# Eight more buffers for modulation weights, a later zero fill, an earlier query projection, and expert lists made beside expert blocks

## The chip, the cores and the metric

The kernel runs on one core of a Trainium2 chip. A core has a matrix engine (TensorE, here PE), a vector engine (DVE), a scalar engine (ACT), a general engine (GpSimd, here POOL) and an engine that mostly issues transfers (SyncE, here SP); sixteen DMA engines move data for all of them. Each engine works through its own list of instructions in order and waits where an operand, a buffer or a transfer is not ready. The metric is device time in microseconds of one execution, lower is better. The kernel before takes 1429.2 us, the median of three runs (1427.99 to 1431.35).

## The reference

One block of a diffusion model with a context prefix: 512 latent and 256 context tokens of width 1024, all in fp32. A conditioning vector gives scales and shifts for each token stream:

```
m = silu(cvec) @ w[:, : n * D_MODEL] + b[: n * D_MODEL]
```

The normalised and modulated tokens are projected by one wide matrix to keys, values, queries, gates and decays. Two mixers run on them, both in both directions of the sequence, and each starts from the state that the context leaves: a retention with a fixed decay per head, and a gated DeltaNet in chunks of 128, which passes the projections through a convolution of three taps and solves a unit lower triangular system in every chunk:

```
a = jnp.einsum('bhnid,bhnjd->bhnij', kc, kc) * bc * jnp.where(strict, jnp.exp(jnp.where(strict, rel, 0.0)), 0.0)
rhs = jnp.concatenate([bc * vc, bc * jnp.exp(g)[..., None] * kc], axis=-1)
sol = lax.linalg.triangular_solve(a + jnp.eye(CHUNK, dtype=a.dtype), rhs,
                                  left_side=True, lower=True, unit_diagonal=True)
```

The merged result goes through an output projection. Then a second normalisation, a router that picks 8 of 64 experts for each token (from 4 of 8 groups), the experts (gate, up and down matrices of width 256), and a shared expert whose output is added.

## The kernel before

Every fp32 product is made of three matmuls, from a high and a low part of each operand (mm3, lines 110 to 113: L111 high by high, L112 and L113 with the low parts). A weight that comes from memory is cast to its high part (hi_of: L100 on ACT, L102 on POOL) and subtracted for its low part (lo_of, L107 on DVE or POOL). Five parts follow one another in the program: the modulation and norms (phase0), the projections and the DeltaNet (phaseG), the retention and the merge (phaseR), the output projection and the router (phaseO), and the experts (phaseM).

The program text is not the order on the engines: a scheduler takes the instructions, puts each on its engine as early as it thinks its operands and buffers are there, and inserts the waits. A buffer is freed by its last reader; a transfer also waits for an earlier one that uses the same completion counter. The counters serve the transfers of SP and ACT in turn.

phase0 loads sixteen pieces of the modulation matrix, wm, 512 KB each (L300, SP), into five buffers. phaseG then casts the projection weights (raw to wu), projects the retention's keys and values from the context (hTc; results rcA and rcB), the gates (gT, L434) and the DeltaNet's keys (kx, kc), which go through conv. The solution of the triangular systems is built by prep, chunk by chunk (CT, M), then by a long chain of small DVE steps for all chunks at once (L569 to L577), written to memory (zd) with zeros where its blocks do not reach, and read back as Z (L582, used at L586). zd is filled with zeros by one transfer (L382) from a small tile.

phaseM holds the experts. Each expert's block on PE is 48 matmuls for gate and up, transposes of the gathered tokens for later experts, and 8 down matmuls (L1258). Weights come three experts ahead. Each expert takes up to 64 tokens in its own slot list; the tokens above 64 go to further lists. Ranks (posm, over, ext) say which tokens those are, and extra makes the first of these lists from them by one-hot matmuls (L1370) with the columns colx. Both are made ahead of the loop over experts.

Of the kernel before, what the change touches and what calls it, by code (L numbers as in the profile page):

```python
# [71 lines left out]
class K:  # L72
# [128 lines left out]
    def run(self, upto="end"):  # L201
        nc, tc, a = self.nc, self.tc, self.a
        main = self.main = self.pool("main")
        self.pes = ExitStack()
        self.psum = self.pool("ps", es=self.pes, space=PSUM)
        self.wi = a["w_in"][0].rearrange("(k p) n -> p k n", p=128)
        self.ident = main.tile([128, 128], F32, name="ident")
        self.mhalf = main.tile([128, 1], F32, name="mhalf")
        nc.vector.memset(self.mhalf, -0.5)
        self.vecT = main.tile([128, 68], F32, name="vecT")  # L210
# [12 lines left out]
        p = self.pool("hcp", side="right", es=self.hcs)  # L223
        self.hTc = p.tile([128, 8, 256], F32R, name="hTc")
        self.hLc = p.tile([128, 8, 256], F32R, name="hLc")
        self.phase0()
        if upto == "0":
            for s in (self.hcs, self.gcs, self.hxs, self.pes):
                s.close()
            return  # L230
        self.phaseG()
        self.phaseR()
        if upto == "R":
            self.w8s.close()
            self.hxs.close()
            self.pes.close()
            return
        self.phaseO()
        self.phaseM()


    def phase0(self):
# [84 lines left out]
        for k in range(8):  # L327
# [6 lines left out]
            self.lo_of(self.hLc[:, k], h, self.hTc[:, k])  # L334
        for k in range(8):
# [10 lines left out]
    def phaseG(self):  # L346
# [87 lines left out]
        nc.scalar.copy(gT[:, 0:512], px[0:16])  # L434
# [54 lines left out]
        def conv(b, dx, dc):  # L489
            cv = lambda j: self.vecT[:, 24 + j * 12 + b:25 + j * 12 + b]  # L490
            r = self.projT({0: 3088, 1: 1024, 2: 1536}[b // 4] + (b % 4) * 128, ctx=dc is not None, lo="dve" if b // 4 == 1 else "pool")
# [35 lines left out]
        for dr in range(2):  # L527
            ps = self.pc()
            brd = gc.tile([128, 6, 4], F32, name="brd", bufs=2)
            nc.vector.tensor_copy(brd, br[:, :, dr * 4:dr * 4 + 4])  # L530
            nc.tensor.transpose(ps[0:24, 0:128], brd.rearrange("p t h -> p (t h)"), self.ident)
            bt = gc.tile([24, 128], F32, name="bt", bufs=2)
            nc.scalar.copy(bt, ps[0:24, 0:128])
            nc.sync.dma_start(bd[dr], bt)

# [164 lines left out]
        for t in range(6):  # L700
            prep(t)
# [10 lines left out]
        for h in range(4):  # L712
            conv(8 + h, vx[:, h], vc[:, h])
        for t in range(6):
# [10 lines left out]
        for h in range(4):  # L725
            conv(h, qx[:, h], None)
# [422 lines left out]
    def phaseM(self):  # L1149
# [156 lines left out]


        r1 = cst("r0")
        tlt, oneb = p.tile([128, 128], BF, name="tlt"), p.tile([128, 128], BF, name="oneb")
        ts(tlt, r1, cst("pidx")[:, 0:1], None, op0=OP.is_gt)  # L1310
        nc.gpsimd.memset(oneb, 1.0)
        f = lambda x: x.rearrange("p c e -> p (c e)")
        ps = self.pi()
        for t in range(4):
            if t > 1:
                nc.tensor.matmul(ps[:, t * 64:t * 64 + 64], oneb, selb[:, t - 2], start=True, stop=False)
            nc.tensor.matmul(ps[:, t * 64:t * 64 + 64], tlt, selb[:, t], start=t < 2, stop=True)
        pc = self.pi()
        for c in (0, 2, 1, 3):
            nc.tensor.matmul(pc[:, c % 2 * 64:c % 2 * 64 + 64], oneb, selb[:, c], start=c < 2, stop=c > 1)  # L1320

        over = p.tile([128, 2, 64], F32, name="over")
        ts(f(over), pc[:, 0:128], -64.0, 0.0, op0=OP.add, op1=OP.max)
        for t in range(4):
            s = slice(t * 64, t * 64 + 64)
            if t % 2:
                nc.vector.scalar_tensor_tensor(posm[:, t], ps[:, s], 65.0, over[:, 0], op0=OP.add, op1=OP.add)
            else:
                ts(posm[:, t], ps[:, s], 65.0, None, op0=OP.add)
        nc.vector.scalar_tensor_tensor(f(sel), ps[:, 0:256], 63.5, f(sel), op0=OP.is_gt, op1=OP.mult)  # L1330
        tt(f(posm), f(posm), f(sel), op=OP.mult)
        ts(f(posm), f(posm), -1.0, None, op0=OP.add)

        ext, rem = p.tile([128, 64], F32, name="ext"), p.tile([128, 64], F32, name="rem")
        tt(rem, over[:, 0], over[:, 1], op=OP.add)
        ts(ext, rem, 0.5, None, op0=OP.is_gt)
        for c in (128.5, 256.5):
            nc.vector.scalar_tensor_tensor(ext, rem, c, ext, op0=OP.is_gt, op1=OP.add)
        nc.vector.tensor_copy(rem, ext)
        nxf, nx = p.tile([128, 1], F32, name="nxf"), p.tile([1, 1], I32, name="nx")  # L1340
        nc.vector.tensor_reduce(nxf, ext, axis=AX.X, op=OP.add)
# [30 lines left out]
        def extra():  # L1372
# [27 lines left out]
            fill(colx, wx[:, :, None], 1)  # L1400
            ps = self.pi()
# [37 lines left out]
        with tc.For_i(0, cnt) as _:  # L1439
            wi, ix, ws = extra()  # L1440
# [51 lines left out]
```

## Time and profile before

| | before |
|---|---|
| median of 3 runs | 1429.2 us |
| profiled execution | 1428.32 us, span 1426.5 |
| mean granted clock of PE | 0.972 |
| PE busy | 1334.9 us (94%) |
| DVE busy | 901.3 us (63%) |
| ACT busy | 654.1 us (46%) |
| POOL busy | 404.4 us (28%) |
| moved by DMA | 340.51 MB, mean 239 GB/s |

The profile is of one execution. Its span lies 1.8 us under that execution's own time. An engine's busy time is what it worked, whether or not anything waited for it; what sets the end is read from the waits of the engine that is full. The granted clock is a share of TensorE's full 2.4 GHz; at 0.5 a matmul takes twice as long. In timelines the number in brackets is the idle time ahead of an instruction, with what ended it; "x2" behind an instruction says that the row stands for two like it.

### The profile page before, as it was taken

What the parts mean: (1) busy time and instruction counts of PE and PEld (TensorE: products, weight loads), DVE (VectorE), ACT (ScalarE), POOL (GpSimd) and SP (SyncE); (2) the same over time, 40 slices, a digit from 0 to 9 for tenths busy, and PEclk for the clock granted to TensorE, in tenths of its full rate; (3) what the DMA queues carried; (4) which work ended last, traced back from release to release, by engine and by line L of the source; (5) the groups of instructions that cost most, each with busy time, mean ns of one, the idle gap of its engine ahead of it and who ended that gap; (6) DMA issues with size and microseconds to landing.
All of it is one profiled execution on the core that took longest, in us unless ns stands there. A gap on an engine that the chain in (4) does not pass through costs nothing.

```text
span 1426.5 us, 20707 instructions
## 1 busy us (share of the span) xinstructions
PE 1334.9 (94%) x7848; PEld 1081.8 (76%) x7848; DVE 901.3 (63%) x1269; ACT 654.1 (46%) x926; POOL 404.4 (28%) x330
## 2 busy tenths in 40 slices
PE   6989888899999999999989999999999999999990
PEld 2658777898887777777878787888888787878770
DVE  5635696457676556547676666666666666666643
ACT  5634431553333222334445555565655555555531
POOL 0313644865320000012402222222222222223312
PEclk9899998999999999999999999999999999999995
DMA  8643521202326578575889999999999999999954
GB/s 291 187 111 104 132 59 27 59 16 80 81 56 181 173 218 233 149 244 198 302 305 339 355 367 342 369 348 354 363 361 358 362 371 350 367 355 360 314 182 126
DMA packets 138841, 340.51 MB, mean 239 GB/s; under 512 B 28218, under 2 KB 84574, under 8 KB 113780
## 3 DMA queue, kind: packets, MB, share of 16 engines
q1 hardware_dynamic: 110952, 289.46, 57.1%
q0 software_dynamic: 19584, 38.99, 10.8%
q10 hardware_dynamic: 8204, 10.72, 2.5%
q8 instruction: 63, 1.03, 0.3%
q14 instruction: 38, 0.31, 0.1%
HBM read 326.59 MB, written 48.31 MB: 263 GB/s over the span
## 4 chain that ended last, share of the span: by engine, by line
PE 46%; DMA 5%; DVE 1%; POOL 1%; issue 0%; ACT 0%; DVEq 0%; SPq 0%; POOLq 0%; ACTq 0%
PE cs L1258 15%; PE acc L112 8%; PE acc L111 8%; PE acc L113 8%; PE ci L1227 4%; DMA wd<-in_w_down_dram 2%; PE ci L1057 2%; DMA wgu<-in_w_up_dram 1%; PE acc L1247 1%; PE acc L1069 1%; DMA w<-acc 1%; POOL fr L127 0%; DMA acc<-y,sl_i 0%; DMA acc<-y,slots 0%; PE ci L1010 0%
## 5 line engine op out<-in xcount | busy, mean ns | idle before, releaser
L111 PE MATMUL acc<-wh,xT 128*128 128x256 f32 x1040 | 305.2, 293 | 0.0
L113 PE MATMUL acc<-wh,xT 128*128 128x256 f32 x1040 | 294.7, 283 | 0.0
L112 PE MATMUL acc<-wl,xT 128*128 128x256 f32 x1040 | 294.4, 283 | 0.0
L1164 DVE TENSOR_TENSOR wl<-w,wh 128x2048 fp32r<-128x2048 f32 x88 | 201.5, 2292 | 87.8 <-PE acc L112 87.7
L1263 POOL DMA_INDIRECT acc<-y,slots x64 | 101.9, 1592 | 479.8 <-ACT y L1260 430.2
L1258 PE MATMUL cs<-wd,aT 128*128 128x512 f32 x520 | 234.3, 593 | 3.3 <-DMA wd<-in_w_down_dram 2.2
L1162 ACT CAST wh<-w 128x2048 fp32r<-128x2048 f32 x88 | 167.2, 1902 | 94.4 <-PE acc L113 76.3
L111 PEld LDWEIGHTS acc<-wh,xT 128*128 128x128 f32 x1040 | 199.9, 192 | 0.2 <-issue 0.2
L112 PEld LDWEIGHTS acc<-wl,xT 128*128 128x128 f32 x1040 | 199.7, 192 | 0.2 <-issue 0.2
L113 PEld LDWEIGHTS acc<-wh,xT 128*128 128x128 f32 x1040 | 199.2, 191 | 0.0
L1258 PEld LDWEIGHTS cs<-wd,aT 128*128 128x128 f32 x520 | 93.9, 190 | 97.3 <-issue 94.7
L1230 DVE TENSOR_TENSOR xT<-ci,xT 128x512 fp32r<-128x512 f32 x130 | 89.3, 687 | 89.7 <-ACT xT L1229 86.2
L100 ACT CAST wu<-raw 128x1024 fp32r<-128x1024 f32 (+1 forms) x73 | 74.9, 1036 | 110.3 <-DMA raw<-in_w_in_dram 76.2
L1164 DVE TENSOR_TENSOR wl<-wgu,wh 128x2048 fp32r<-128x2048 f32 x42 | 96.3, 2292 | 42.7 <-PE acc L112 41.5
L111 PE MATMUL acc<-hTx,wu 128*128 128x512 f32 (+1 forms) x296 | 119.3, 403 | 1.8 <-ACT wu L100 1.8
L113 PE MATMUL acc<-hTx,wu 128*128 128x512 f32 (+1 forms) x296 | 118.3, 400 | 1.6 <-DVE wu L107 1.6
L112 PE MATMUL acc<-hLx,wu 128*128 128x512 f32 (+1 forms) x296 | 117.9, 398 | 0.0
L107 DVE TENSOR_TENSOR wu<-raw,wu 128x1024 fp32r<-128x1024 f32 (+1 forms) x61 | 77.5, 1277 | 62.8 <-ACT wu L100 62.8
L1162 ACT CAST wh<-wgu 128x2048 fp32r<-128x2048 f32 x42 | 79.7, 1898 | 53.8 <-PE acc L113 36.5
L1227 PEld LDWEIGHTS ci<-ident,xg 128*128 128x128 f32 x520 | 73.6, 192 | 29.9 <-issue 29.5
L1219 POOL DMA_INDIRECT xg<-h2d,slots x64 | 71.5, 1117 | 35.6 <-issue 18.3
L1227 PE MATMUL ci<-ident,xg 128*128 128x128 f32 x520 | 80.4, 279 | 0.0
(492 smaller groups left out, 2362.4 us busy)
## 6 DMA issues: line engine op xcount, KB each, us to landing
wd<-in_w_down_dram SPq DMA_DIRECT2D x64, 1024.0 KB
w<-in_w_gate_dram SPq DMA_DIRECT2D x43, 1024.0 KB
w<-in_w_up_dram SPq DMA_DIRECT2D x43, 1024.0 KB
raw<-in_w_in_dram SPq DMA_DIRECT2D x56, 512.0 KB
wgu<-in_w_gate_dram SPq DMA_DIRECT2D x21, 1024.0 KB
wgu<-in_w_up_dram SPq DMA_DIRECT2D x21, 1024.0 KB
mraw<-in_w_mod_dram SPq DMA_DIRECT2D x32, 512.0 KB
wm<-in_w_mod_dram SPq DMA_DIRECT2D x16, 512.0 KB
```

Source lines behind the costliest of these rows:

```text
L100: nc.scalar.copy(dst, src)
L107: (self.nc.gpsimd if eng == "pool" else self.nc.vector).tensor_tensor(dst, src, hi.bitcast(F32), op=OP.subtract)
L111: mm(out, ah, bh, start=start, stop=False)
L112: mm(out, ah, bl, start=False, stop=False)
L113: mm(out, al, bh, start=False, stop=stop)
L1162: nc.scalar.copy(h[:, i:i + max(n, 1024)], w[:, i:i + max(n, 1024)])
L1164: eng(l[:, i:i + n], w[:, i:i + n], h[:, i:i + n].bitcast(F32), op=OP.subtract)
L1219: nc.gpsimd.indirect_dma_start(xg[:, :], None, self.h2d[:, :], bass.IndirectOffsetOnAxis(ap=ix, axis=0), bounds_check=511, oob_is_err=False)
L1227: nc.tensor.transpose(ps[:, k * 128:k * 128 + 128], xv[:, :, c * 4 + k], self.ident)
L1230: tt(l, ps, h.bitcast(F32), op=OP.subtract)
L1258: nc.tensor.matmul(ps, aT[:, m], wd[:, s], start=k == 0, stop=k == 1)
L1263: nc.gpsimd.indirect_dma_start(self.accd[acc][:, :], bass.IndirectOffsetOnAxis(ap=sx, axis=0), y[:, :], None, bounds_check=511, oob_is_err ...
```

## The change

Four things. First, eight of the sixteen pieces wm get a place of their own, in the memory of the tiles hTx and hLx (which are now made later, in that same memory); the other eight share the three buffers of rawp. Second, the zero fill reads a wider stretch of zeros, 774 columns instead of 258, and is issued behind ACT's copy of the gates. Third, the two brd transposes come behind the first two of six calls of prep, and the DeltaNet's first query projection (q0) comes ahead of the transposes of the values. Fourth, the ranks are made in the expert loop at e == 3, the columns of the further list at e == 5, and the list itself at e == 7.

```diff
-        self.hTx = p.tile([128, 8, 512], F32R, name="hTx", tag="b0")
-        self.hLx = p.tile([128, 8, 512], F32R, name="hLx", tag="b1")
...
+        wms = [t[:, i] for t in [self.hxpool.tile([128, 4, 1024], F32, name="wm", tag=tag) for tag in ("b0", "b1")] for i in range(4)]
         for k in range(8):
             for hf in range(2):
                 i = k * 2 + hf
-                w = (self.rawp if i % 5 < 3 else wp).tile([128, 1024], F32, name="wm", tag="raw")
+                w = wms[i - 3] if 3 <= i < 11 else self.rawp.tile([128, 1024], F32, name="wm", tag="raw")
                 nc.sync.dma_start(w, wv[:, k, hf * 1024:hf * 1024 + 1024])
...
+        self.hTx = self.hxpool.tile([128, 8, 512], F32R, name="hTx", tag="b0")
+        self.hLx = self.hxpool.tile([128, 8, 512], F32R, name="hLx", tag="b1")
...
-        zero = gp.tile([128, 258], F32, name="zero", tag="E")
+        zero = gcv[:, 2:4].rearrange("p a n -> p (a n)")[:, 0:774]
         nc.gpsimd.memset(zero, 0.0)
-        nc.scalar.dma_start(zd.rearrange("t h n -> (t h n)").rearrange("(p a n) -> p a n", p=128, n=258), zero[:, None, :].to_broadcast([128, 12, 258]))
...
-        nc.scalar.copy(gT[:, 0:512], px[0:16])
+        with tc.issue_after(nc.scalar.copy(gT[:, 0:512], px[0:16]).ins):
+            nc.scalar.dma_start(zd.rearrange("t h n -> (t h n)").rearrange("(p a n) -> p a n", p=128, n=774), zero[:, None, :].to_broadcast([128, 4, 774]))
...
+        def conv_in(b, ctx):
+            return self.projT({0: 3088, 1: 1024, 2: 1536}[b // 4] + (b % 4) * 128, ctx=ctx, lo="dve" if b // 4 == 1 else "pool")
...
-        for dr in range(2):
-            ps = self.pc()
-            brd = gc.tile([128, 6, 4], F32, name="brd", bufs=2)
...
-        for t in range(6):
+        prep(0)
+        prep(1)
+        for dr in range(2):
+            ps = self.pc()
+            brd = gc.tile([128, 6, 4], F32, name="brd", bufs=2)
...
+        for t in range(2, 6):
             prep(t)
...
         for h in range(4):
             conv(8 + h, vx[:, h], vc[:, h])
+        q0 = conv_in(0, False)
         for t in range(6):
             pk = self.pc()
...
-            conv(h, qx[:, h], None)
+            conv(h, qx[:, h], None, q0 if h == 0 else None)
...
+        def ranks():
...
-        def extra():
+        def extra_cols():
...
+            return wi, px, colx
+
+        def extra_list(wi, px, colx):
             ps = self.pi()
             pv = ps[:, 0:6].rearrange("p (e j) -> p e j", e=1)
             onehot_mm(pv[:, 0], lambda c: px[:, c:c + 1], lambda c: colx[:, c, 0])
...
-        self.xtra = extra()
         x = lambda e: [XT[e][:, h] for h in range(2)]
         for e in range(NE + 2):
+            if e == 3:
+                ranks()
+            if e == 5:
+                xcols = extra_cols()
+            if e == 7:
+                self.xtra = extra_list(*xcols)
```

The body of ranks is what stood ahead of the loop, word for word. The loop for lists beyond the first, behind the experts, calls extra_list(*extra_cols()) where it called extra().

How the change moves instructions, at three places. On ACT around the zero fill, before; wu are weights being cast, rcA and rcB results of the retention's context projections, gT the gates:

```order
L100 CAST wu<-raw 128x1024 [waits DMAHW1_49]
L100 CAST wu<-raw 128x1024 [waits DMAHW2_49,PE_49]
L382 DMA zd<-zero 1536x1x258 [waits Pool_49]
L415 COPY rcA<-acc 128x512 [waits PE_49] x2
L100 CAST wu<-raw 128x1024 [waits DMAHW3_49]
L100 CAST wu<-raw 128x1024 [waits DMAHW5_49,DVE_49]
L100 CAST wu<-raw 128x128 [waits DMAHW6_49,DVE_49,PE_49]
L415 COPY rcB<-acc 128x512 [waits PE_49] x2
L434 COPY gT<-acc 16x512 [waits PE_49]
L435 COPY gT<-acc 16x256 [waits PE_49]
```

The same place on ACT after the change:

```order
L417 COPY rcA<-acc 128x512 [waits DVE_49,PE_49]
L100 CAST wu<-raw 128x1024 [waits DMAHW3_49]
L100 CAST wu<-raw 128x1024 [waits DMAHW4_49,DVE_49,PE_49]
L100 CAST wu<-raw 128x128 [waits DMAHW5_49,DVE_49,PE_49]
L100 CAST wu<-raw 128x1024 [waits DMAHW6_49,DVE_49,PE_49]
L417 COPY rcB<-acc 128x512 [waits PE_49,Pool_49]
L417 COPY rcB<-acc 128x512 [waits PE_49]
L100 CAST wu<-raw 128x1024 [waits DMAHW7_49,DVE_49]
L436 COPY gT<-acc 16x512 [waits PE_49]
L437 DMA zd<-gcv 512x1x774
L438 COPY gT<-acc 16x256 [waits PE_49]
```

The fill has moved from between the weight casts to behind the first gT copy, and two more weight casts stand ahead of rcB and gT.

On PE at the end of the value convolutions, before; gcv holds their results, and the matmuls with ident transpose them:

```order
L113 MATMUL acc<-hTc,wu 128x256
L717 MATMUL cs<-ident,gcv 128x128 x2
L717 MATMUL cs<-ident,gcv 128x128 [waits Activation_49]
L717 MATMUL cs<-ident,gcv 128x128 x3
L111 MATMUL acc<-hTx,wu 128x512
```

The same place on PE after the change:

```order
L113 MATMUL acc<-hTc,wu 128x256
L111 MATMUL acc<-hTx,wu 128x512 [waits DVE_49,Activation_49]
L112 MATMUL acc<-hLx,wu 128x512
L113 MATMUL acc<-hTx,wu 128x512 [waits Pool_49]
...
L113 MATMUL acc<-hTx,wu 128x512
L726 MATMUL cs<-ident,gcv 128x128 x2
L726 MATMUL cs<-ident,gcv 128x128 [waits Activation_49] x2
```

A whole projection of 24 matmuls now stands between the last value projection and the transposes.

On PE around the one-hot matmuls of the further list, before; wd and aT belong to a down projection, xg holds gathered tokens:

```order
L1258 MATMUL cs<-wd,aT 128x512 x3
L1370 LDWEIGHTS oh [waits DVE_49]
L1370 MATMUL ci<-colx,oh 128x6 [waits PE_49]
L1370 LDWEIGHTS oh
L1370 MATMUL ci<-colx,oh 128x6
L1227 MATMUL ci<-ident,xg 128x128 [waits DMASW3_49]
```

After the change, the ranks in the block e == 3 (tlt and oneb are constants) and the one-hot matmuls in the block e == 7:

```order
L1267 MATMUL cs<-wd,aT 128x512 x3
L1236 MATMUL ci<-ident,xg 128x128 [waits DVE_49,PE_49]
L1236 MATMUL ci<-ident,xg 128x128 x3
L1331 LDWEIGHTS tlt
L1331 MATMUL ci<-selb,tlt 128x64 [waits DVE_49]
...
L1334 LDWEIGHTS oneb [waits DVE_49]
L1334 MATMUL ci<-selb,oneb 128x64 [waits PE_49]
...
L1382 MATMUL ci<-colx,oh 128x6 [waits DVE_49]
...
L1382 LDWEIGHTS oh [waits DVE_49]
L1382 MATMUL ci<-colx,oh 128x6
```

The ranks' matmuls stand behind the transposes of a block, and the one-hot matmuls some four blocks later; in both places PE waits for DVE in order.

## Rows read from the trace of the kernel before

**Rows 1.** Page, busy time: engine, busy us, share of span, instructions.

```profile
PE 1334.9 (94%) x7848; PEld 1081.8 (76%) x7848; DVE 901.3 (63%) x1269; ACT 654.1 (46%) x926; POOL 404.4 (28%) x330
```

**Rows 2.** Windows: stretch, length, busy of five engines, granted clock, DMA share, GB/s.

```profile
0.00:40.00 40.00, 27.78 (x98) 8.12 (x98) 20.62 (x29) 20.95 (x28) 2.19 (x7) 1.00 0.87 303
70.00:75.00 5.00, 3.50 (x15) 2.47 (x14) 0.00 (x0) 0.00 (x0) 0.00 (x0) 1.00 1.09 185
75.00:85.00 10.00, 6.54 (x21) 4.96 (x22) 1.43 (x2) 2.41 (x4) 1.16 (x2) 0.66 0.64 166
85.00:100.00 15.00, 13.35 (x85) 8.70 (x83) 5.59 (x17) 3.64 (x8) 2.95 (x3) 1.00 0.00 1
100.00:130.00 30.00, 30.00 (x169) 25.85 (x168) 16.69 (x35) 13.15 (x23) 7.53 (x6) 1.00 0.50 141
185.00:200.00 15.00, 10.70 (x46) 8.77 (x45) 14.55 (x22) 7.05 (x12) 5.77 (x4) 0.77 0.13 38
725.00:745.00 20.00, 16.04 (x84) 12.93 (x85) 14.67 (x42) 8.32 (x11) 2.67 (x2) 0.83 0.66 233
765.00:1385.00 620.00, 617.78 (x3946) 502.61 (x3945) 405.94 (x356) 353.01 (x414) 160.75 (x119) 1.00 0.98 349
```

**Rows 3.** Waits of SP, 0 to 40 us: us in total, times, longest.

```profile
SPq L300 <- DVE wmu L107: 7.7, 8, 1.8
SPq L300 <- DMA tri<-in_cst_dram: 4.5, 1, 4.5
```

**Rows 4.** Timeline of ACT, 60 to 80: start, us, operation, idle before and releaser.

```profile
63.01 0.58 ACTq L382 DMA_DIRECT2D zd<-zero  x1
...
76.90 1.24 ACT L100 CAST wu<-raw 128x1024 fp32r<-128x1024 f32 x2 [10.32 <-DMA raw<-in_w_in_dram]
```

**Rows 5.** Timeline of PE, 72 to 84, projections from hTc.

```profile
72.87 0.40 PE L112 MATMUL acc<-wu,hTc 128*128 128x512 f32 x1
73.10 0.40 PE L113 MATMUL acc<-wu,hLc 128*128 128x512 f32 x1
77.99 0.79 PE L111 MATMUL acc<-wu,hTc 128*128 128x512 f32 x1 [4.50 <-ACT wu L100]
...
83.69 0.44 PE L113 MATMUL acc<-wu,hLc 128*128 128x512 f32 x1
```

**Rows 6.** Timeline of ACT, 90 to 96.

```profile
94.13 0.57 ACT L434 COPY gT<-acc 16x512 f32<-16x512 f32 x1 [9.39 <-PE acc L113]
```

**Rows 7.** Timeline of PE, 97 to 99.

```profile
97.34 0.54 PE L439 MATMUL cs<-ident,gT 16*128 16x16 f32 x6 [0.45 <-ACT gT L435]
98.29 0.50 PE L111 MATMUL acc<-hTx,wu 128*128 128x512 f32 x1 [0.41 <-ACT wu L100]
```

**Rows 8.** Timeline of PE, 143 to 150, the two transposes of brd.

```profile
146.19 0.27 PE L531 MATMUL cs<-ident,brd 128*24 128x128 f32 x1 [2.16 <-DVE brd L530]
...
149.24 0.37 PE L531 MATMUL cs<-ident,brd 128*24 128x128 f32 x1 [1.62 <-DVE brd L530]
```

**Rows 9.** Timeline of PE at 191 and at 249.

```profile
191.23 0.69 PE L717 MATMUL cs<-ident,gcv 128*128 128x128 f32 x2 [4.30 <-ACT gcv L501]
...
249.42 0.63 PE L586 MATMUL ci<-ident,Z 128*128 128x128 f32 x4 [1.76 <-DMA Z<-zd]
```

**Rows 10.** Lines of DVE, 176.4 to 242.5: operation, count, busy us, mean ns.

```profile
L574 DVE TENSOR_TENSOR tmp<-N,W 96x62 f32<-96x62 f32 (+15 forms) x31 | 20.7, 668 | 0.8
```

**Rows 11.** Waits of DVE, 176 to 250.

```profile
DVE XR L592 <- DMA Z<-zd: 6.9, 1, 6.9
...
DVE N L569 <- DMA M<-cd: 1.9, 1, 1.9
```

**Rows 12.** Timeline of PE, ahead of the expert loop.

```profile
732.62 0.21 PE L1370 MATMUL ci<-colx,oh 128*128 128x6 bf16 x2 [3.91 <-DVE colx L1356]
```

**Rows 13.** Timeline of DVE, the same place: one weight subtraction.

```profile
729.05 2.28 DVE L1164 TENSOR_TENSOR wl<-w,wh 128x2048 fp32r<-128x2048 f32 x1
```

**Rows 14.** Lines of PE in the expert loop, 765 to 1385.

```profile
L1258 PE MATMUL cs<-wd,aT 128*128 128x512 f32 x480 | 216.1, 593 | 2.2 <-DMA wd<-in_w_down_dram 2.2
```

More of the change, by code (lines that the diff above doesn't have):

```diff
@@ L209, in run @@
         nc.vector.memset(self.mhalf, -0.5)
+        self.eps = main.tile([128, 1], F32, name="eps")
+        nc.vector.memset(self.eps, EPS)
         self.vecT = main.tile([128, 68], F32, name="vecT")
@@ L486, in phaseG, with conv @@
         nc.scalar.activation(kts, kts, AF.Exp)
[L489 removed]
+        def conv_in(b, ctx):
+            return self.projT({0: 3088, 1: 1024, 2: 1536}[b // 4] + (b % 4) * 128, ctx=ctx, lo="dve" if b // 4 == 1 else "pool")
+        def conv(b, dx, dc, r=None):
             cv = lambda j: self.vecT[:, 24 + j * 12 + b:25 + j * 12 + b]
[L491 removed]
+            if r is None:
+                r = conv_in(b, dc is not None)
             for ps, dst, n in ((r, dx, 512),) if dc is None else ((r[0], dx, 512), (r[1], dc, 256)):
@@ L698, in step @@
                     ptt(o, o, bj(c), op=OP.mult)
-        for t in range(6):
+        prep(0)
[3 more added lines that the diff above has]
+            brd = gc.tile([128, 6, 4], F32, name="brd", bufs=2)
+            nc.vector.tensor_copy(brd, br[:, :, dr * 4:dr * 4 + 4])
+            nc.tensor.transpose(ps[0:24, 0:128], brd.rearrange("p t h -> p (t h)"), self.ident)
+            bt = gc.tile([24, 128], F32, name="bt", bufs=2)
+            nc.scalar.copy(bt, ps[0:24, 0:128])
+            nc.sync.dma_start(bd[dr], bt)
+        for t in range(2, 6):
             prep(t)
@@ L1308, in phaseM @@
         r1 = cst("r0")
[L1309 to L1329, printed above, removed]
@@ new lines, in phaseM @@
+        nx = p.tile([1, 1], I32, name="nx")
+        g2p = self.keep.tile([128, 1024], F32, name="g2p", tag="k1")
+        def ranks():
+            tlt, oneb = p.tile([128, 128], BF, name="tlt"), p.tile([128, 128], BF, name="oneb")
+            ts(tlt, r1, cst("pidx")[:, 0:1], None, op0=OP.is_gt)
+            nc.gpsimd.memset(oneb, 1.0)
+            f = lambda x: x.rearrange("p c e -> p (c e)")
+            ps = self.pi()
+            for t in range(4):
+                if t > 1:
+                    nc.tensor.matmul(ps[:, t * 64:t * 64 + 64], oneb, selb[:, t - 2], start=True, stop=False)
+                nc.tensor.matmul(ps[:, t * 64:t * 64 + 64], tlt, selb[:, t], start=t < 2, stop=True)
+            pc = self.pi()
+            for c in (0, 2, 1, 3):
+                nc.tensor.matmul(pc[:, c % 2 * 64:c % 2 * 64 + 64], oneb, selb[:, c], start=c < 2, stop=c > 1)
+            over = p.tile([128, 2, 64], F32, name="over")
+            ts(f(over), pc[:, 0:128], -64.0, 0.0, op0=OP.add, op1=OP.max)
+            for t in range(4):
+                s = slice(t * 64, t * 64 + 64)
+                if t % 2:
+                    nc.vector.scalar_tensor_tensor(posm[:, t], ps[:, s], 65.0, over[:, 0], op0=OP.add, op1=OP.add)
+                else:
+                    ts(posm[:, t], ps[:, s], 65.0, None, op0=OP.add)
+            nc.vector.scalar_tensor_tensor(f(sel), ps[:, 0:256], 63.5, f(sel), op0=OP.is_gt, op1=OP.mult)
+            tt(f(posm), f(posm), f(sel), op=OP.mult)
+            ts(f(posm), f(posm), -1.0, None, op0=OP.add)
+            tt(rem, over[:, 0], over[:, 1], op=OP.add)
+            ts(ext, rem, 0.5, None, op0=OP.is_gt)
+            for c in (128.5, 256.5):
+                nc.vector.scalar_tensor_tensor(ext, rem, c, ext, op0=OP.is_gt, op1=OP.add)
+            nc.vector.tensor_copy(rem, ext)
+            nxf = p.tile([128, 1], F32, name="nxf")
+            nc.vector.tensor_reduce(nxf, ext, axis=AX.X, op=OP.add)
+            ts(nxf, nxf, -1.0, 0.0, op0=OP.add, op1=OP.max)
+            nc.vector.tensor_copy(nx, nxf[0:1])
+            nc.sync.dma_start(g2p, self.modd[3:4].to_broadcast([128, 1024]))
@@ L1439, in phaseM @@
         with tc.For_i(0, cnt) as _:
-            wi, ix, ws = extra()
+            wi, ix, ws = extra_list(*extra_cols())
             xT, xg = xtile(), gather(ix)
```

18 lines of the change are left out of this document (removed).

## The prediction

> **What bounds the kernel now.** I read the page first: TensorE (PE) is busy 1334.9 of 1426.5 us, so a change is worth what it takes out of PE's 91.6 idle us or out of stretches at the lower clock [rows 1]. The table by stage comes next; the reader is to see in it where PE is full whatever the others do (100 to 130 us: 30.00 of 30; the expert loop from 765: 617.78 of 620) and where it is not: the first 40 us, 70 to 100, 185 to 200 and 725 to 745 [rows 2]. A saving ahead of a full stretch is carried through it unchanged. Then the timelines of those places, for the instruction that PE waited for. All sums are against the profiled execution, 1428.3 us, 0.9 under the median of the three runs (1429.2).
>
> **Part 1, eight more buffers for the modulation weights.** In the first 40 us SP, which issues the sixteen 512 KB loads, waits 7.7 us for the subtractions that free a buffer, but also 4.5 us in one piece for an unrelated transfer (tri) that it must see done before it issues the next [rows 3]. DMA is busy .87 of this window, so no more than .13 x 40 = 5.2 us of transfer time can be won [rows 2]. The change lets eight loads go without a freed buffer; the waits of the second kind stay. Nothing is taken off PE. I take half the bound, 2.5 us, range 0 to 5.2. The tiles hTx and hLx are only made when these eight loads have been read; their first writer runs behind the whole modulation, so I cost that at nothing (0 to 1 us if wrong).
>
> **Part 2, the zero fill.** ACT issues it at 63.01, between the weight loads of the hTc projections [rows 4]. It moves 1548 KB in 1536 rows of 1032 B, by its shape. ACT's next weight cast but one then waits 10.32 us for its load and starts at 76.90 [rows 4]; DMA is busy past full in 70 to 75 and yet moves only 185 GB/s, against 303 at .87 in the first 40 us [rows 2]. PE stands 4.50 us before the matmul at 77.99, and then works at its lower clock level, 1.2 GHz, for a while: 75 to 85 has a granted clock of .66, which is .34 x 2 x 10 = 6.8 us at that level [rows 2, 5]. Full-clock matmuls of this shape start 0.23 apart (72.87, 73.10); from 73.10 to 83.69 lie 12 of them, which is 2.8 us, and 10.6 us passed: 7.8 late [rows 5]. Some of it comes back as the ordinary wait for the cast and subtraction of the same tiles, so I take 7.0, range 5 to 7.8. The fill now stands behind ACT's first copy gT, which ran at 94.13 [rows 6]. There DMA is idle: 85 to 100 has a share of 0.00 [rows 2]. If the fill is as slow as before (63.01 to about 76, the end of ACT's wait, 13 us) it ends near 107, beside the loads of 100 to 130 at a share of .50; loss 0 to 2 us, taken as 0, as these loads leave half the DMA free. The Trainium skill ("DMA: Bandwidth & Descriptors", Specifications) puts the smallest transfer for line rate at 512 B, by which rows of 1032 B would be at full rate already and the new rows of 3096 B would win nothing. The trace does not agree, by the 185 GB/s beside 303 [rows 2]; by the rule the fill would still last its 13 us, and the sum would be worse by the 0 to 2 just named.
>
> The same reordering puts ACT's casts for the first key projection ahead of rcB and gT (first pieces of the order). PE's waits there, .45 for gT and .41 for the weights, are what it can win: 0.9 us, range 0 to 0.9 [rows 7].
>
> **Part 3, the brd transposes behind prep(0) and prep(1).** Two PE waits of 2.16 and 1.62 us go [rows 8]. What is late next: PE now comes some 4 us earlier to the chunk products (L551), which need a buffer that DVE frees, and on which it was queued behind these two waits before. So two waits become one. I take 0; bounds -1 (one more cast now stands ahead on ACT) to +3.8.
>
> **Part 4, the first query projection ahead of the value transposes.** PE waits 4.30 us for ACT at 191.23, and 185 to 200 has a clock of .77 [rows 2, 9]. Now 24 matmuls 0.23 apart, 5.5 us, stand in that place (second pieces of the order). But PE does not end this stage. DVE is busy 14.55 of these 15 us [rows 2]: from 176.4 to 242.5 it runs 31 of L574, 20.7 us, and as many of L575 at the same price [rows 10]. Then W is stored and Z loaded from it: PE waits 1.76 us for Z at 249.42, and DVE 6.9 for the same transfer [rows 9, 11]. A PE that is earlier waits longer there. I take 0. Bounds: -1 (a longer idle before Z and a lower clock behind it) to +6 (4.30 and, by the .77, .23 x 15 / 2 = 1.7 of clock).
>
> **Part 5, ranks and further lists.** Before, they stand ahead of the expert loop: DVE works through some forty short instructions (of ranks and extra, in the code) among its weight subtractions of 2.28 us [rows 13], and PE waits 3.91 us for colx and resumes at 732.62 [rows 12]. 725 to 745 has a mean clock of .83, so .17 x 2 x 20 = 6.8 us lay at the lower level, which costs half of it, 3.4, where PE had work [rows 2]: with the wait 7.3, less about .1 for the start of it, 7.2. Now ranks stand in block 3, the columns in block 5, the list in block 7 (third pieces of the order). 620 us of the loop hold 480 down matmuls, eight a block, so 60 blocks of 10.3 us [rows 14]; DVE is busy 405.94/60 = 6.8 in each, 3.5 free [rows 2]. The forty instructions, all shorter than the 2.28 of a subtraction and mostly a tenth of it, are about 10 us over five blocks. The small matmuls are those of before, but at two places PE now waits in order for a psum buffer or a one-hot tile from DVE: some 1 us each, by less than one such subtraction in between; 0 if DVE is ahead, and the 3.91 of before if it is behind. 7.2 - 2 = 5.
>
> Against it stands the weight stream: DMA is busy .98 over the loop [rows 2]. But it had time to spare just because of the stall: in 725 to 745 its share is .66, .34 x 20 = 6.8 us idle [rows 2]. A stream that no longer idles there can end as much earlier. I take 5, range 0 to 7.2.
>
> **Sum.** 2.5 + 7.0 + 0.9 + 0 + 0 + 5 = 15.4, and 1428.3 - 15.4 = 1412.9: 1413. By the median it would be 0.9 more, which I leave to the range.
>
> **Rivals.** (A) The loop gives nothing: DMA's share of .98 is the real bound, and each early block is paid back at the end by waits for wd, of which there are now only 2.2 us [rows 14]. For it the share, against it the 6.8 idle us above. 1428.3 - 10.4 = 1418.
> (B) The early gain is lost in the base chain: if what starts DVE's chain at 176.4, the load of M that it waits 1.9 us for [rows 11], does not move because it hangs on POOL and ACT rather than PE, parts 1 and 2 end as PE wait before Z, and 5 is left: 1423. Against it: the key projections from which M is made sit in the full stretch from 100 on.
> (C) Slower, by in-order waits in the loop. Each of the three pieces lands between a down projection and the next block's matmuls, where PE would stop as at 732.62 [rows 12]. Three stops with their clock cost 3 x 7.2 = 21.6 against 7.2 removed: 1428.3 - 10.4 + 14.4 = 1432. It decides from (10.4 + 7.2)/3 = 5.9 us per stop. For it speaks that colx did just this once; against it that DVE now has free time in a block before each is asked for. The Trainium skill ("TensorE: Matmul & The Clock Gate", HAM oscillation — how this bites in real kernels) says that a wait which returns in every tile drops the clock each time and its cost is paid each time; the trace shows such a drop here once, at .83.
> (D) The base chain follows PE, and part 4 pays its 6 too: 1407.
> (E) The new buffers do nothing, since SP's other waits pace it: 1415, inside the forecast.
>
> **Chances.** Forecast 0.57 (with E), its own range 1407 to 1420; A 0.17, B 0.09, D 0.09, C 0.08. The range leaves out C and the ends: 1405 to 1424. A measurement of this kernel tells no less than 0.2%, 2.9 us, from no change; forecast, A and D lie beyond it, B but for its upper edge: faster 0.88, same 0.04, slower 0.08.
>
> **What would show it.** In the profile after: no wait of PE over 1 us in 70 to 85, and full clock there; the fill on DMA behind 85; the key projections ending some 10 us earlier; PE's wait before Z longer than 1.76, not shorter (else D); blocks 3 to 7 of the loop near 10.3 us, none over 12 (else C); waits for wd no larger than now (else A). The forecast is wrong if PE reaches Z less than 8 us earlier, or if the loop's blocks grow.

## The result, and the profile after

The changed kernel takes 1408.4 us, the median of six runs (1404.7 to 1415.9), against 1429.3 before. The ratio is 0.9862, 95% interval 0.9836 to 0.9887: 20.9 us faster, where 15.4 were forecast. It lies in the range (1405 to 1424), near its lower end, and just inside the 1407 to 1420 that the likeliest case had to itself. Rival D's 1407 is nearer to it than the forecast's 1413; whether D's reason holds is for the experiments.

One thing must be known to read the profile. Executions of the changed kernel spread over 11 us, and the profiled one is the slowest of them, 1415.9 us. So the trace shows 12.4 of the 20.9 us. This execution also had the lowest mean granted clock of the six: 0.971, against 0.976 to 0.979 in the other five. From the difference, 0.005 to 0.008 x 2 x 1414 is 14 to 23 us more at the lower clock level, which costs up to half of that, 7 to 11 us; that is about what it was late.

The page after, its line of busy times:

```profile
PE 1324.8 (94%) x7848; PEld 1074.7 (76%) x7848; DVE 906.7 (64%) x1270; ACT 653.4 (46%) x926; POOL 409.6 (29%) x330
```

PE did the same 7848 matmuls in 10.1 us less busy time [rows 1]. The clock did not give that, as its mean is 0.971 where it was 0.972; the matmuls themselves must lie closer somewhere. The stretches of [rows 2] again, after:

```profile
0.00:40.00 40.00, 25.96 (x91) 8.23 (x92) 20.05 (x30) 20.00 (x26) 4.08 (x9) 0.96 0.80 278
70.00:75.00 5.00, 5.00 (x24) 4.14 (x23) 1.56 (x3) 1.25 (x2) 0.00 (x0) 1.00 0.70 180
75.00:85.00 10.00, 9.41 (x57) 7.26 (x56) 5.39 (x11) 3.19 (x4) 4.87 (x4) 1.00 0.73 178
85.00:100.00 15.00, 15.00 (x92) 11.05 (x91) 5.86 (x22) 4.62 (x9) 0.00 (x0) 1.00 0.48 163
100.00:130.00 30.00, 29.54 (x181) 26.12 (x181) 15.30 (x29) 13.33 (x24) 9.19 (x8) 1.00 0.38 107
185.00:200.00 15.00, 14.35 (x66) 11.94 (x67) 14.59 (x17) 5.36 (x9) 8.35 (x6) 0.89 0.24 71
725.00:745.00 20.00, 20.00 (x136) 15.99 (x135) 16.85 (x24) 12.12 (x15) 5.40 (x4) 1.00 0.98 364
765.00:1385.00 620.00, 611.94 (x3925) 493.65 (x3923) 403.38 (x360) 350.28 (x414) 164.84 (x119) 1.00 0.97 345
```

70 to 100 and 725 to 745 are at full clock and, but for 0.6 us, full: the two stalls are gone. The first 40 us are not better: DMA .80 and 278 GB/s, where they were .87 and 303.

Where the time came from, by the start of the same matmul or cast in three traces (the last column is a later experiment, an execution of 1406.1 us of the same kernel without parts 3 and 4):

| the same instruction | before | after minus before | e11 minus before |
|---|---|---|---|
| last matmul of the modulation | 39.31 | +2.3 | -0.2 |
| ACT's first copy gT | 94.13 | -5.3 | -8.0 |
| first value result vx (ACT) | 150.51 | -7.2 | -9.5 |
| first transpose of Z | 249.42 | -3.2 | -8.6 |
| first down projection | 725.01 | +0.9 | -8.8 |
| second expert's down projection | 744.15 | -7.9 | -17.7 |
| 53rd expert's | 1270.46 | -13.2 | -23.0 |
| last down projection | 1393.06 | -12.2 | -21.5 |

In e7, another later experiment, which keeps part 4, it is -7.3 at the first down projection, -21.4 at the 53rd and -20.7 at the last. So there are four pieces: 7 to 9 us ahead of the first experts, 8.8 at the lists, 5.3 that come little by little in the expert loop, and 0.7 to 1.5 given back at its end. The third was not in the forecast at all.

### The profile page after: what moved, and what is told of

The parts are those of the page before. It is cut to its first block, busy times and chain, and to the rows that moved or that the text cites. A ratio compares the mean times of both kernels' runs of the same rounds, so it can differ in the third digit from the quotient of the medians.

```text
span 1414.1 us, 20716 instructions
## 1 busy us (share of the span) xinstructions
PE 1324.8 (94%) x7848; PEld 1074.7 (76%) x7848; DVE 906.7 (64%) x1270; ACT 653.4 (46%) x926; POOL 409.6 (29%) x330
## 3 DMA queue, kind: packets, MB, share of 16 engines
q0 software_dynamic: 19584, 38.99, 10.9%
## 4 chain that ended last, share of the span: by engine, by line
PE 43%; DMA 7%; issue 1%; ACT 1%; POOL 1%; DVE 0%; DVEq 0%; SPq 0%; ACTq 0%; POOLq 0%
PE cs L1267 13%; PE acc L111 7%; PE acc L113 7%; PE acc L112 7%; DMA w<-in_w_up_dram 4%; PE ci L1236 3%; DMA w<-in_w_gate_dram 2%; PE ci L1066 2%; PE acc L1078 1%; PE acc L1256 1%; DMA w<-acc 1%; POOL fr L127 0%; DMA acc<-y,slots 0%; DMA acc<-y,sl_i 0%; ACT wh L1171 0%
## 5 line engine op out<-in xcount | busy, mean ns | idle before, releaser
L111 PE MATMUL acc<-wh,xT 128*128 128x256 f32 x1040 | 302.2, 291 | 0.0
L113 PE MATMUL acc<-wh,xT 128*128 128x256 f32 x1040 | 291.0, 280 | 0.0
L112 PE MATMUL acc<-wl,xT 128*128 128x256 f32 x1040 | 290.6, 279 | 0.0
L111 PEld LDWEIGHTS acc<-wh,xT 128*128 128x128 f32 x1040 | 196.6, 189 | 0.2 <-issue 0.2
L112 PEld LDWEIGHTS acc<-wl,xT 128*128 128x128 f32 x1040 | 196.1, 189 | 0.2 <-issue 0.2
L113 PEld LDWEIGHTS acc<-wh,xT 128*128 128x128 f32 x1040 | 195.5, 188 | 0.0
L112 PE MATMUL acc<-hLx,wu 128*128 128x512 f32 (+1 forms) x296 | 117.1, 396 | 0.0
L1228 POOL DMA_INDIRECT xg<-h2d,slots x64 | 75.5, 1180 | 35.6 <-issue 18.0
```

Of the source, the lines that this page charges most:

```text
L111: mm(out, ah, bh, start=start, stop=False)
L112: mm(out, ah, bl, start=False, stop=False)
L113: mm(out, al, bh, start=False, stop=stop)
L1228: nc.gpsimd.indirect_dma_start(xg[:, :], None, self.h2d[:, :], bass.IndirectOffsetOnAxis(ap=ix, axis=0), bounds_check=511, oob_is_err=False)
```

## The experiments

### The changed kernel again (e0)

No edit.

> The changed kernel once more, nothing edited, for a second profile: the first one is of an execution of 1415.9 us, while the median is 1408.4. In it the modulation ended 2.3 us later than before, Z was read only 3.2 us earlier, and the first down projection came 0.9 us later. Theory 1 (that execution was late at the start, in phase 0, and the rest is as shown): this profile has the modulation's last matmul near or before 39.3, and everything behind it some 4 to 7 us earlier than in the first profile, 1404 to 1410 us. Theory 2 (the start is always 2.3 us late, and the executions differ somewhere behind Z): the last modulation matmul at 41 to 42 again, and the difference appears after 246 us.

1405.7 us (1403.8 to 1414.0, five runs), ratio 0.9843 [0.9820, 0.9866]. The profiled execution is again the slowest, 1414.0, and much like the first: modulation at 41.08, Z at 245.48, first down projection at 724.73. Theory 1 falls for the profiles. Theory 2 has the late start right, but later profiles of near kernels are ahead of these two before Z already. What tells the executions apart on record is the clock again: 0.972 in this one, 0.975 to 0.978 in the four that took 1403.8 to 1408.1.

One place where the executions part can be seen. In the retention's end PE waits 1.67 us for DVE, after, and the clock then drops; first the row, then the window:

```profile
641.31 1.09 PE L1128 MATMUL ci<-ident,h 128*128 128x128 f32 x8 [1.67 <-DVE h L1119]
```

```profile
640.00:650.00 10.00, 8.68 (x35) 7.55 (x36) 7.10 (x22) 3.62 (x6) 2.91 (x3) 0.66 0.59 209
```

The same two in the kernel of e1, an execution of 1407.1 us, with the same wait:

```profile
636.80 1.09 PE L1127 MATMUL ci<-ident,h 128*128 128x128 f32 x8 [1.67 <-DVE h L1118]
```

```profile
640.00:650.00 10.00, 10.00 (x57) 8.36 (x56) 8.76 (x35) 4.01 (x9) 3.36 (x4) 1.00 0.44 163
```

One and the same wait costs the lower level for .34 x 2 x 10 = 6.8 us, 3.4 us of work, in one execution and nothing in the other. The kernel before had the wait (1.68) and the full clock in its profile. That is part of the spread; which execution gets it, no run here tells.

### Part 1 undone (e1), and phase 0 alone (e8, e9)

```diff
-                w = wms[i - 3] if 3 <= i < 11 else self.rawp.tile([128, 1024], F32, name="wm", tag="raw")
+                w = (self.rawp if i % 5 < 3 else wp).tile([128, 1024], F32, name="wm", tag="raw")
```

> The changed kernel with the sixteen modulation weights in the five old buffers again. Theory 1 (part 1 gains 2.5 us as forecast): 2 to 3 us slower than the changed kernel, 1411. Theory 2 (the eight buffers only move SP's wait to the last two loads, which still go through three buffers; the first profile shows the modulation 2.3 us later): 2 us faster, 1406. Theory 3 (part 1 is worth nothing on average): same within 1 us.

1409.1 us (1407.1 to 1416.0), ratio 0.9879 [0.9854, 0.9904], against e0's 1405.7 on the same chip: 3.4 us slower, with intervals that overlap. By the times it is nearest to theory 1. The modulation ends at 39.37 in its profile. With the new buffers it ends at 41.1 to 41.6 in three profiles (after, e0, e3), which have a granted clock of 0.96 in the first 40 us, and at 37.9 to 39.6 in six others (e2, e5 to e7, e10, e11), which have 1.00. To part the two, phase 0 by itself:

```diff
-            K(ctx, tc, aps, out).run()
+            K(ctx, tc, aps, out).run("0")
```

> Phase 0 alone (modulation, norms, hTc, hTx), with the eight more buffers; everything behind it is left out, and hTx is stored as the output in place of the block's result. Measures part 1 by itself, in executions without the whole program behind them. Theory 1 (forecast: 2.5 us gained): 2 to 3 us shorter than the same with the old buffers. Theory 2 (the last two loads, which still go through three buffers, end later: in four profiles with the new buffers the modulation ends at 41 us, in four others at 38 to 39.6, and with the old ones at 38.2 to 39.4): 0 to 2 us longer, with a wider spread.

> Phase 0 alone with the five old buffers, everything behind it left out and hTx stored as the output. Theory 1: 2 to 3 us longer than with the new buffers. Theory 2: the same or up to 2 us shorter, with a narrower spread.

65.71 us (64.80 to 65.97) with the new buffers and 65.76 (65.57 to 66.50) with the old; as ratios to one kernel 0.0457 [0.0455, 0.0459] and 0.0461 [0.0460, 0.0462]. So the buffers themselves are worth 0.05 us by the medians and 0.6 by the ratios, not 2.5, and both theories miss. SP's waits, 0 to 40 us after, show why:

```profile
SPq L301 <- DMA wm<-in_w_mod_dram: 8.9, 2, 6.1
SPq L301 <- DMA tri<-in_cst_dram: 4.5, 1, 4.5
SPq L301 <- DVE wmu L107: 4.1, 3, 2.7
```

The 7.7 us of waits for subtractions [rows 3] have become 4.1, but 8.9 us of waits for earlier wm loads have come, in two pieces, and tri's 4.5 stayed. In phase 0 by itself the sum does not move at all; e8, then e9:

```profile
SPq L302 <- DMA wm<-in_w_mod_dram: 11.0, 7, 6.1
SPq L302 <- DVE wmu L107: 5.4, 2, 4.4
```

```profile
SPq L303 <- DVE wmu L107: 12.8, 11, 3.0
SPq L303 <- DMA wm<-in_w_mod_dram: 3.6, 1, 3.6
```

11.0 + 5.4 and 12.8 + 3.6 are both 16.4 us. The wait moved from the buffers to the loads in flight. Whether part 1 is worth the other 3 us of e1 in the whole program stays open.

### Part 2 undone (e2)

```diff
+        zero = gp.tile([128, 258], F32, name="zero", tag="E")
         nc.gpsimd.memset(zero, 0.0)
+        nc.scalar.dma_start(zd.rearrange("t h n -> (t h n)").rearrange("(p a n) -> p a n", p=128, n=258), zero[:, None, :].to_broadcast([128, 12, 258]))
```

> The changed kernel with the zero fill in its old place and with its short rows. Theory 1 (7.0 us as forecast, carried unchanged to the end): PE's stall near 75 us is back with about 4.5 us, 1415. Theory 2 (the base chain of DVE and POOL takes part of every early gain; in the first profile 5.3 us at gT have become 3.2 at Z): only 3 to 4 us slower, 1412, and PE waits less for Z.

1419.3 us, ratio 0.9934 [0.9909, 0.9958]: 13.6 us slower than e0, 10.9 than the six runs. The timeline of PE has the stall again, of the old size:

```profile
76.58 0.79 PE L111 MATMUL acc<-wu,hTc 128*128 128x512 f32 x1 [4.41 <-ACT wu L100]
```

Slower than either theory said. Take the time from the last hTx cast (64.66 in after, 60.99 in e2, 62.11 before). To gT (88.85, 92.17, 94.13) it is 24.2 us after the change, 31.2 in e2 and 32.0 before: the stall was worth 7.0 to 7.8, as forecast. To the fourth key result kx (123.91, 130.44, 130.74) it is 59.3, 69.5 and 68.6: 10.2 more in e2, and 9.4 more before. Of e2's 3.2 behind gT, 1.1 are the waits of .45, .41 and .28 at 95 to 98 us that it has again and the changed kernel has not. Another 1.7 is the clock, which falls behind these waits in e2 alone:

```profile
98.00:102.00 4.00, 4.00 (x13) 3.09 (x12) 3.86 (x12) 3.35 (x4) 0.00 (x0) 0.57 0.83 209
```

That is .43 x 2 x 4 = 3.4 us at the lower level; before, the clock is 1.00 from 85 to 130 [rows 2], and behind gT it takes 1.6 us more than after. So against the kernel before part 2 is worth 9.4 us, where the forecast had 7.0 + 0.9; what makes up the rest of e2's 13.6 is not shown. The fill itself, in the trace of after, issued at 88.86:

```profile
88.00:90.00 2.00, 2.00 (x16) 1.36 (x15) 0.00 (x0) 0.58 (x1) 0.00 (x0) 1.00 0.00 0
90.00:92.00 2.00, 2.00 (x17) 1.69 (x16) 0.00 (x0) 0.41 (x2) 0.00 (x0) 1.00 0.97 382
92.00:94.00 2.00, 2.00 (x11) 1.63 (x10) 0.00 (x0) 0.90 (x1) 0.00 (x0) 1.00 1.02 396
94.00:96.00 2.00, 2.00 (x14) 1.44 (x13) 0.96 (x3) 0.70 (x4) 0.00 (x0) 1.00 0.07 22
```

4 us at 382 to 396 GB/s, with rows of 3096 B and nothing beside it. So the loss of 0 to 2 us kept for a slow fill was nothing. The old fill had the DMA engines nearly to itself as well. In the trace of before, the queues of ACT (q10, the fill) and SP (q1, the loads) from 65 to 71 us, in packets, MB and share of the 16 engines, and a window inside:

```profile
q10 hardware_dynamic: 1267, 1.31, 109.1%
q1 hardware_dynamic: 14, 0.01, 0.7%
```

```profile
68.00:70.00 2.00, 2.00 (x10) 1.63 (x9) 0.00 (x0) 0.00 (x0) 0.00 (x0) 1.00 1.15 143
```

Sixteen engines at 143 GB/s take 16 x 1032 / 143 = 115 ns for a row of 1032 B, and at 389 GB/s 16 x 3096 / 389 = 127 ns for a row of 3096 B: by this estimate a row costs about the same at either length. So the old fill was slow by itself, and not by the loads, which came behind it; what it had of its own is the short rows, and the small tile that they were read from. Only at its start did it move 355 GB/s (65 to 66 us); why not longer is not shown. The rule of the Trainium skill weighed in the prediction ("DMA: Bandwidth & Descriptors", Specifications: line rate from 512 B on) gave the other answer; the measurement, 143 GB/s with rows of 1032 B and 382 to 396 with rows of 3096, decides against it. No run moved the fill without widening its rows, so what the later place is worth alone stays open.

### Part 5 undone (e3)

```diff
+        self.xtra = extra()
         x = lambda e: [XT[e][:, h] for h in range(2)]
         for e in range(NE + 2):
-            if e == 3:
-                ranks()
```

> The changed kernel with ranks and the further list ahead of the expert loop again. Theory 1 (5 us as forecast: 7.2 of stall and clock less 2 for waits in the blocks): 1413, PE's stall of about 4 us before the one-hot matmuls is back. Theory 2 (first profile: 8.8 us between the first and the second down projection, and then blocks that are 0.12 us shorter from block 8 on, 5 us more by block 52, of which 1 is lost to waits for weights): 13 us slower, 1421. Theory 3 (shorter blocks are not from the lists): 8 to 9 us slower, 1417, and the blocks are still 10.2 us.

1415.4 us, ratio 0.9915 [0.9892, 0.9937]: 9.7 us over e0, 7.0 over the six runs. The stall on PE is back:

```profile
731.39 0.21 PE L1379 MATMUL ci<-colx,oh 128*128 128x6 bf16 x2 [3.90 <-DVE colx L1365]
```

By its blocks theory 3 is the one that holds, and the time lies between 1 and 3. What the ranks cost inside block 3, in the timeline of after:

```profile
740.13 0.22 PE L1331 MATMUL ci<-selb,tlt 128*128 128x64 bf16 x2
...
740.30 0.28 PE L1334 MATMUL ci<-selb,oneb 128*128 128x64 bf16 x4
740.42 0.36 PE L111 MATMUL acc<-wh,xT 128*128 128x256 f32 x1
```

From 740.13 to 740.42, 0.3 us, and no wait ahead of any. From the second expert's down projection to the eighth's, the six blocks that hold all three pieces, it is 61.96 us, 0.75 more than six plain blocks of 10.20. Rival C's three stops are not there, and the 2 us I set aside were too many. The blocks of e3 are 10.19 us as well, from the first on. So theory 2 falls: the shorter blocks are not from the lists.

### The tile that nothing reads (e4, e5, e10)

What e1, e2 and e3 share with the changed kernel, and the kernel before has not, is small: the moves of parts 3 and 4, and the tile eps, a fifth thing in the change, which the four things named ahead of the prediction leave out.

```diff
+        self.eps = main.tile([128, 1], F32, name="eps")
+        nc.vector.memset(self.eps, EPS)
```

e4 is the kernel before with these two lines, e5 the changed kernel without them.

> The kernel before with one line pair of the change alone: the tile eps of one column, which nothing reads, and its memset. In the profiles so far the blocks of the expert loop take 10.20 us in every kernel that has this tile (with the lists undone as well) and 10.31 in the kernel before; the difference is in the 48 gate and up matmuls, 0.1206 against 0.1229 us apart. In the built program the tile moves the tiles behind it by 32 bytes, among them the expert weights wh and wl that these matmuls read (75136 to 75168, 91520 to 91552), while xT stays. Theory 1 (the place of wh and wl sets this): blocks of 10.20 us, 64 x 0.115 = 7.4 us faster than before, 1421. Theory 2 (the shorter blocks come from the reordered early part, by another state of the clock or the DMA): no change, 1428, blocks 10.31.

> The changed kernel without the tile eps. Theory 1 (the place of the weights): blocks of 10.31 us again, 6 to 7 us slower than the changed kernel, 1415. Theory 2 (something else in the change): as the changed kernel, 1408, blocks 10.20.

e4: 1420.5 us, ratio 0.9955 [0.9940, 0.9970], 6.4 us faster than before. e5: 1415.1, ratio 0.9894 [0.9864, 0.9924], 6.7 us slower than the changed kernel by the medians, 4.6 by the ratios, with intervals that overlap: two of its six executions took 1407.4 and 1407.5, as the changed kernel does. They were not profiled. By the blocks, 10.19 us in e4 and 10.32 in e5, theory 1 holds in both, and two unread lines are worth nearly as much as the lists. The same stretch of the loop, PE full in each: before, then e4, then e5, a window and its row of L112:

```profile
800.00:1250.00 450.00, 450.00 (x2892) 367.68 (x2891) 298.74 (x261) 260.94 (x307) 115.61 (x88) 1.00 1.00 359
```

```profile
L112 PE MATMUL acc<-wl,xT 128*128 128x256 f32 x704 | 198.9, 282 | 0.0
```

```profile
800.00:1250.00 450.00, 450.00 (x2920) 365.72 (x2919) 303.05 (x265) 264.57 (x309) 117.19 (x89) 1.00 1.00 362
```

```profile
L112 PE MATMUL acc<-wl,xT 128*128 128x256 f32 x709 | 197.9, 279 | 0.0
```

```profile
800.00:1250.00 450.00, 450.00 (x2883) 366.84 (x2882) 299.50 (x260) 261.73 (x305) 114.57 (x88) 1.00 1.00 359
```

```profile
L112 PE MATMUL acc<-wl,xT 128*128 128x256 f32 x700 | 197.9, 283 | 0.0
```

The reader is to see three nanoseconds in the mean, 282 and 283 against 279, at the same granted clock, and 28 matmuls more in the same full 450 us. By their starts, the matmuls of 256 columns lie 0.1231 us apart without the tile and 0.1206 with it; 48 in a block, 10.32 against 10.20 us. The eight down matmuls of a block take 3.44 in both.

Is it a place in a pitch of 64 bytes?

```diff
-        self.eps = main.tile([128, 1], F32, name="eps")
+        self.eps = main.tile([128, 16], F32, name="eps")
```

> The changed kernel with the unread tile eps of sixteen columns, 64 bytes, in place of one column: in the built program the expert weights wh and wl are moved by 32 bytes more, to 75200 and 91584, again a multiple of 64 as in the kernel before, and xT stays. Theory 1 (what counts is where the weights lie in a pitch of 64 bytes): blocks of 10.31 us and 1415 us, as without the tile. Theory 2 (any move away from the old place helps, or the place against xT): blocks of 10.20 and 1408.

1413.1 us, ratio 0.9903 [0.9887, 0.9918]: slower than the changed kernel, by 4.7 us, but its blocks are 10.25 us, with 0.1215 between matmuls. Neither theory fits: a multiple of 64 again is not as slow as before, and not as fast as the changed kernel. The memset of eps is the same single instruction in e10 and in the changed kernel, so it is not what sets the blocks. That the size of this unread tile decides, and with it the place of the tiles behind it, is shown; which of these tiles counts, and which property of the place, is open.

### Parts 3 and 4 undone (e7, e6, e11)

e6 puts the query projection back behind the value transposes, e7 the brd transposes back ahead of prep; e11 does both.

```diff
             conv(8 + h, vx[:, h], vc[:, h])
-        q0 = conv_in(0, False)
...
+        for dr in range(2):
+            ps = self.pc()
+            brd = gc.tile([128, 6, 4], F32, name="brd", bufs=2)
...
         ZT, QE, CTs = {}, {}, {}
```

> The changed kernel with the first query projection behind the value transposes again. Theory 1 (forecast: DVE's chain ends this stage, so q0 is worth nothing): same within 2 us; PE waits about 4 us before the transposes and less before Z. Theory 2 (q0 turns one wait into a longer one: in the profiles PE waits 5.0 us before the product of qx and kx, where it was 2.95, and 2.4 for a weight on POOL): faster by 1 to 3 us, since Z comes earlier. Theory 3 (rival D): 4 to 6 us slower.

> The changed kernel with the brd transposes ahead of prep again. Theory 1 (forecast: two waits became one of the same size; the profile shows one of 3.88 us): same within 1.5 us, with two PE waits of about 2 and 1.6 us. Theory 2 (the transposes held up PE for the longer part): 2 to 4 us slower.

> The changed kernel with both moves of part 3 and 4 undone: the brd transposes ahead of prep, the first query projection behind the value transposes; buffers, fill, lists and the tile eps stay. Theory 1 (q0 costs at Z what the single profiles show, 3 us, and the weight stream, which fills the DMA engines in the expert loop, takes about half of any earlier start back): Z at 239 to 240, blocks of 10.20 us, more waits for weights behind block 52, 1405, about 2 us under the changed kernel. Theory 2 (the ends are held by the stream alone): within 1 us of 1407, as with one of the two undone.

e6 1409.5 us, ratio 0.9874 [0.9852, 0.9897]; e7 1406.7, 0.9858 [0.9835, 0.9882]; e11 1406.6, 0.9873 [0.9852, 0.9894]. All three intervals hold the changed kernel's 0.9862: the two moves are worth nothing that can be told, as forecast, and e11's time goes with its theory 2. In e7 the two waits for brd are back (2.22 and 0.79 us), in place of the first wait below. On the way, q0 is not harmless. PE's waits of this stage, after:

```profile
143.34 0.49 PE L551 MATMUL ci<-kx 128*128 128x128 f32 x2 [3.88 <-DVE CT L553]
...
185.65 1.33 PE L726 MATMUL cs<-ident,gcv 128*128 128x128 f32 x5 [2.73 <-ACT gcv L508]
...
213.83 2.08 PE L747 MATMUL ci<-qx,kx 128*128 128x128 f32 x8 [5.01 <-ACT qx L508]
230.84 0.50 PE L112 MATMUL acc<-wu,hTx 128*128 128x512 f32 x1 [2.39 <-POOL wu L107]
246.23 0.63 PE L584 MATMUL ci<-ident,Z 128*128 128x128 f32 x4 [2.76 <-DMA Z<-zd]
```

and in e6:

```profile
181.96 0.44 PE L725 MATMUL cs<-ident,gcv 128*128 128x128 f32 x2 [4.73 <-ACT gcv L508]
208.27 1.16 PE L746 MATMUL ci<-qx,kx 128*128 128x128 f32 x8 [1.00 <-ACT qx L508]
215.30 0.94 PE L746 MATMUL ci<-qx,kx 128*128 128x128 f32 x6 [2.47 <-ACT qx L508]
239.49 0.63 PE L584 MATMUL ci<-ident,Z 128*128 128x128 f32 x4 [2.77 <-DMA Z<-zd]
```

With q0 ahead, the wait before the transposes shrinks from 4.73 to 2.73, and one of 5.01 takes its place before the product of qx and kx, with another 2.39 behind. The wait before Z is the same, 2.76 and 2.77. From the last matmul of the modulation to the first transpose of Z it is 210.1 us before, 203.1 to 204.6 in five profiles with q0 ahead (after, e0, e1, e5, e7), and 200.5 and 201.7 without (e6, e11): q0 costs 1.4 to 4.1 us at Z. But little of that reaches the end. At the 53rd expert e6 is 2.8 us ahead of e7, which keeps q0, and at the last 1.3, with the weight stream full; and by the medians e6 is the slower one.

## Why the prediction was right, point by point

**Direction and range: right.** The stages that were read as lossy (70 to 100 us and the lists) were, and their loss was removed and carried to the end.

**Part 1: the term was mis-sized.** "I take half the bound, 2.5 us": phase 0 alone shows 0 to 0.6. That was case E, "since SP's other waits pace it", inside the forecast. The bound of 5.2 us from the DMA share was sound; half of a bound is not a measurement.

**Part 2: right in mechanism, too small in size.** The fill's 7.0 us were measured as 7.0 (against e2) and 7.8 (against before) up to gT. What the casts ahead of rcB and gT brought was 1.6 against before, not 0.9: a third wait of .30 us, at 99.55, was not in the sum, and 13 matmuls of the key projection now run ahead of the transposes of gT, so that the two named waits were not all that "it can win". The fear of a long fill beside the next loads was needless.

**Part 3: right.** Two waits of 2.16 and 1.62 became one of 3.88, and the time is the same.

**Part 4: right in the sum, only half in the reason.** Q0 gives nothing. PE's wait before Z grew from 1.76 to 2.76 [rows 9], which was named as the sign against rival D, but it is 2.77 without q0 too (e6), so it tells nothing of D. D falls because e6 and e11 undo q0 and are not slower. That the time came out near D's 1407 has other reasons. The longer wait stands before the product of qx and kx, 5.01 where 2.95 stood before, not before Z, and q0 does not only fail to help there: it costs 1.4 to 4.1 us at Z. From 210 to 220 the granted clock is .50:

```profile
210.00:220.00 10.00, 6.17 (x26) 5.88 (x27) 9.80 (x15) 2.66 (x4) 3.08 (x2) 0.50 0.01 2
```

DVE is full there (9.80 of 10) and sets the pace, as said. The Trainium skill ("TensorE: Matmul & The Clock Gate", HAM oscillation — how this bites in real kernels) tells of waits that drop the clock each time. The trace agrees for the wait of 5.01, in and behind which the lower level stands; a wait of 1.67 at 641 was followed by it in one execution and not in another, so a short wait's price is not one number.

**Part 5: right, too small.** Forecast 5 of 7.2; measured 7.0 to 9.7 by time. The 8.8 of the trace hold 1.3 that was only moved: between the first two down projections stood 20 transposes of gathered tokens, now 8, and the other twelve, 0.11 us each, come ahead of the first one. Counted from the first such transpose (706.51 before, 707.14 after) to the second down projection it is 8.5, less the 0.75 in the blocks. The 2 us of in-order waits were not there, as DVE was ahead each time. Rival A, "each early block is paid back at the end", came in a small way: the row of down matmuls, after, beside [rows 14]:

```profile
L1267 PE MATMUL cs<-wd,aT 128*128 128x512 f32 x488 | 220.1, 594 | 4.5 <-DMA wd<-in_w_down_dram 3.6 <-ACT aT L1258 0.8
```

Waits for wd of 3.6 instead of 2.2 us, and 0.7 to 1.5 us given back from the 53rd expert on (2.2 in e6, which was earliest). "A stream that no longer idles there can end as much earlier" held: 725 to 745 has a DMA share of .98 now.

**Its own signs.** Most came true: no PE wait over 0.6 us and full clock in 70 to 85, the fill behind 85, no block over 10.6 us among the early ones. Two did not. Waits for wd grew. And "the forecast is wrong if PE reaches Z less than 8 us earlier": it does so 3.2 us earlier in the profile after, and 5.5 to 7.0 in the profiles with q0 when counted from the modulation's end. So by its own test the early sum of 10.4 us failed; of its terms, part 1 was too large, and q0's price at Z was taken as nothing.

**What was missing.** The prediction took a block of the loop as 10.3 us before and after and gave the tile eps no word. It was worth 6.4 us alone. With some 5 for it, 15.4 would have been 20, and the 20.9 measured. That this fits so well, and that the time lies in the range at all without this term, is partly luck: part 1 was too large by 2 and part 4 cost some us at Z, parts 2 and 5 were too small by 1.5 and 2 to 3, and the stream took 0.7 to 1.5 back.

## What to carry to other kernels

Compare the spacing of the commonest matmul in both traces before explaining a gain by waits: a difference of 2% there is in no list of stalls, and here it was nearly as large as a stall removed. An edit that adds or resizes a tile moves all tiles behind it, so it is an edit to their places too, and belongs into the list of terms even if no instruction reads it. And work that keeps an engine late once (the lists) can be free when it is spread over blocks in which that engine has time.

## What the runs showed of the hardware that was not expected

- With an unread tile of one column ahead of them, which moves the tiles wh and wl by 32 bytes (75168 in place of 75136, as noted ahead of e4), the matmuls that read these tiles, 256 columns of fp32, start 0.1206 us apart instead of 0.1231, at full clock; with 64 bytes it is 0.1215. Their other operand, xT, did not move.
- One transfer of 1.59 MB from a tile of zeros takes 4 us at 382 to 396 GB/s in rows of 3096 B with the DMA engines free; in rows of 1032 B, nearly alone as well, it started at 355 and fell to 143, with the engines at 1.15 of full.
- The same wait of PE, 1.67 us, is followed by the lower clock level in some executions and not in others of nearly the same program; where it is, 3.4 us of work are lost.
